# A hybrid decoder block on one core: the recurrence's small transfers move to GpSimd's queue, and SyncE carries loads alone in a fixed order

## The chip, the cores and the metric

The kernel runs on one core of one Trainium2 chip. The metric is the device time of one execution in microseconds. Five instruction streams share the core's SBUF: TensorE (PE; PEld are its weight loads), VectorE (DVE), ScalarE (ACT), GpSimd (POOL) and SyncE (SP). SP and POOL issue DMA transfers here; each engine runs its own stream in order, and an instruction whose input isn't there holds all behind it.

## The reference

One decoder block over 512 tokens of width 2048, in float32. What matters for the change:

```python
mod = c_act @ w_ada[l] + b_ada[l]            # six modulation vectors of 2048
h = rmsnorm(x) * (1 + sc1) + sh1
p = h @ w_in[l]                              # r, k, v of 16 heads, low-rank inputs, 1024 pool columns
y_rwkv = rwkv7_mixer(p[..., :N_RWKV_COLS])   # per head and token: S = S*w + (S a) b^T + v k^T;  y = S r
y_pool = pool_mixer(p[..., N_RWKV_COLS:])    # moving averages over 2, 4, 8, 16 tokens, then a 256x256 matrix
x = x + gt1 * (concat(y_rwkv, y_pool) @ w_out[l])
h = rmsnorm(x) * (1 + sc2) + sh2
x = x + gt2 * conv_ffn(h)                    # gated MLP with a causal convolution of width 3
return rmsnorm(x)
```

## The kernel before, in words

**Stages.** Activations lie transposed: 128 features on the partitions, 512 tokens along the row. Weights arrive as 128x512 float32 blocks (256 KB); `split_weights` (L111) loads one on SP (L113), rounds it to a high part on ACT (L115) and forms the low part on DVE (L117). Each product of two 128x128 by 128x512 blocks is three matmuls (high by high, high by low, low by high). The first stage (to about 160 us) computes half of the modulation, the normed input and the first eight of the 35 column blocks of W_in. The second, the *recurrence* stage, is the one that is changed. After it come the output projection, the MLP and the final norm.

**The recurrence stage** interleaves two things on TensorE. The filler is the rest of the projection: 27 column blocks, each 16 products, so 27 x 48 = 1296 matmuls at L333 (`win_units`), one *unit* each. The other is the recurrence of the 16 heads, taken as 8 pairs of heads, in chunks of 64 tokens. A pair goes through `stage_a` (decay, keys, the scores within a chunk), an inversion of small triangular matrices, `stage_b` (the steps over the 8 chunks) and `post` (group norm, bonus, gate). `recurrence` (L688) writes TensorE's order by hand: it keeps a modelled `clock` in us, each part yields what it takes and how long its results need, and where no part is ready a unit of the projection is put in. `manual_schedule` (L734) binds TensorE to that order. The other engines, SP and POOL among them, are ordered by the scheduler of the language.

**The columns of r, k, v.** `win_pair` (L641) makes the three column blocks of the next pair. `shift` (L234) takes each from PSUM to SBUF (one ACT and one DVE instruction), into a `spill` tile that is stored to DRAM (`sp`, L648); `stage_a` loads it again (L387) into tiles of the rings `ring` (7 buffers) and `v`. The first thing that ACT does with them is a square (L395).

**The small inverses.** The scores of a pair (L448, masked on DVE at L450) contain 64 triangular blocks of 16x16. Eight transfers gather them to DRAM (`dn`, L456), one brings them back with one block per partition (`nl`, L458), DVE inverts all 64 together (28 short instructions at L472 and L474, between L466 and L475), one transfer stores the result (`dx`, L477), and eight scatter it (L479) into `x4w`, a buffer that is zeroed once (L339). ACT copies that to `x4` (L482). All of these transfers are issued by SP. `q.inverted` (L483) is the modelled time at which the inverse is there, 44 us on; `stage_b` waits for it (L525) before its first product with the inverse (L530).

**The second part of the modulation** fills DVE: `ada_rest` (L343) loads 192 blocks of 256 KB (L350) into three `war` buffers and reduces each against a piece of c in `cq` (L348) with one DVE instruction (L351); one is traced at every sixth unit.

**The pooling groups** take their sums over tokens on DVE (`pool_front`, L276) and their matrix on TensorE (`pool_back`, L296); results go to DRAM (`mixd`, L305), as those of the pairs do (L636). `load_mix` (L749) reads them in the next stage.

Of the kernel before, what the change touches and what calls it, by code (L numbers as in the profile page):

```python
# [16 lines left out]
P = 128  # L17
# [11 lines left out]
NB = 10  # L29
NJ = NF // 2  # L30
# [27 lines left out]
def block_kernel(ctx, tc, a, out, stop=None, dbg=None):  # L58
# [52 lines left out]
    def split_weights(src, eng=V):  # L111
        raw = wp.tile([P, WC], F32, tag="wraw", name="wraw", bufs=4)
        nc.sync.dma_start(raw, src)  # L113
        hi = wp.tile([P, WC], F32R, tag="whi", name="whi", bufs=3)
        S.copy(hi, raw)  # L115
        lo = wp.tile([P, WC], F32R, tag="wlo", name="wlo", bufs=3)
        eng.tensor_tensor(lo, raw, hi[:, :].bitcast(F32), op=ALU.subtract)  # L117
        return hi, lo
# [7 lines left out]
    def project(ps, src, acts, start=True, stop=True, engs=(V,)):  # L126

        n = len(acts)
        for k0 in range(0, n, WC // P):
            wh, wl = split_weights(src[:, k0 * P : k0 * P + WC], engs[k0 // 4 % len(engs)])  # L130
# [45 lines left out]
    first = {}  # L176
    p0ctx = ExitStack()
    p0 = p0ctx.enter_context(tc.tile_pool(name="p0", bufs=1))
    if True:
# [28 lines left out]
        for k in range(KT):  # L208
# [14 lines left out]
            for i0 in range(0, 8, WC // P):  # L223
                wh, wl = split_weights(a["win0"][k, :, i0 * P : i0 * P + WC])
                for ii in range(WC // P):
                    sl = slice(ii * P, (ii + 1) * P)
                    mm3(pf[i0 + ii], wh[:, sl], wl[:, sl], *H[k], start=k == 0, stop=k == KT - 1)
        p0ctx.close()
# [4 lines left out]
        if True:  # L233
# [8 lines left out]
            def ring16(name):  # L242
                return ra.tile([P, 16 + T], F32, tag="ring", name=name, bufs=7)
# [3 lines left out]
            S.activation(xwa[0:64, :], xwa[0:64, :], AF.Tanh)  # L247
            xg1 = ra.tile([P, T], F32, tag="xg1", name="xg1")
            shift(pf[1], 25, xg1)
            S.activation(xg1, xg1, AF.Sigmoid)  # L250
            xg2 = ra.tile([P, T], F32, tag="xg2", name="xg2")
            shift(pf[2], 26, xg2)
            S.activation(xg2, xg2, AF.Sigmoid)
# [5 lines left out]
            for i, m in ((3, 0), (4, 8), (5, 16)):  # L259
                t = vtile("v") if i == 5 else ring("rkv")  # L260
# [3 lines left out]
            upad = [ring16("upad") for i in range(2)]  # L264
            for i in range(2):
                V.memset(upad[i][:, 0:16], 0.0)
                S.copy(upad[i][:, 16:], pf[6 + i])
            ps0ctx.close()

    def load_pw(gi):  # L270
        t = ra.tile([P, T], F32, tag="war", name="pw", bufs=3)
# [24 lines left out]
    def pool_back(gi, zs, pw):  # L296
        for d in range(2):
# [6 lines left out]
            if gi:  # L304
                nc.sync.dma_start(mixd[8 + j], mx)  # L305
# [16 lines left out]

    def win_units(fi, ps):

        src = a["win1"][fi - 8, :, :]
# [12 lines left out]
    x4w = ra.tile([P, 8, 2, 64], F32, tag="x4", name="x4w")  # L338
    G.memset(x4w, 0.0)  # L339
    cq = [None]  # L340
    modq = ra.tile([P, 4, 48], F32, tag="modq", name="modq")

    def ada_rest(n0, n1):  # L343
        for n in range(n0, n1):
            kq, j = divmod(n, 48)
            if j == 0:
                cq[0] = ra.tile([P, T], F32, tag="cq", name="cq")
                nc.sync.dma_start(cq[0], cact[0:1, kq * T : (kq + 1) * T].partition_broadcast(P))  # L348
            wa = ra.tile([P, T], F32, tag="war", name="war", bufs=3)
            nc.sync.dma_start(wa, a["ada2"][kq, j, :, :])  # L350
            V.scalar_tensor_tensor(wa, wa, 1.0, cq[0], op0=ALU.mult, op1=ALU.mult,  # L351
                                   accum_out=modq[:, kq, j : j + 1])
# [16 lines left out]
    class Pair:  # L369
        begun = False  # L370

# [9 lines left out]
    def stage_a(p, q):  # L381

        if p:
            rkv = []
            for i in range(3):
                t = vtile("v") if i == 2 else ring("rkv")
                nc.sync.dma_start(t, sp[p, i])  # L387
                rkv.append(t)
        else:
            rkv = rkv0  # L390
        r, k, v = rkv
        lw = ra.tile([P, P], F32, tag="lw", name="lw")
        nc.sync.dma_start(lw, a["lora"][p, :, 0, :])
        sq = ring("sq")
        S.activation(sq, k, AF.Square, scale=col("kk", p))  # L395
        yield 0.0, 4.0
# [10 lines left out]
        S.activation(al, psal, AF.Sigmoid, bias=col("a0", p))  # L407
        tc.keep_in_program_order(S.preload_act_table_set("natural_log_exp_and_others"))
# [3 lines left out]
        mid = ra.tile([P, NL, 1], F32, tag="mid", name="mid", bufs=2)  # L412
# [40 lines left out]
        nl = ra.tile([64, 16, 16], F32, tag="nl", name="nl")  # L453
        dn = tc.dram_tile([64, 16, 16], F32, name=f"dn{p}")
        for b in range(8):
            nc.sync.dma_start(dn[8 * b : 8 * b + 8, :, :].rearrange("s i j -> i s j"),  # L456
                              nt[16 * b : 16 * b + 16, :, 16 * (b % 4) : 16 * (b % 4) + 16])
        nc.sync.dma_start(nl, dn[:, :, :])  # L458
# [5 lines left out]
        V.scalar_tensor_tensor(k2, r, col("rk", p), k2, op0=ALU.mult, op1=ALU.mult)  # L464
        xyl = ra.tile([64, 2, 16, 16], F32, tag="xyl", name="xyl")
        V.tensor_add(xyl[:, 1, :, :], nl, lanei)  # L466
        prod = ra.tile([64, 64], F32, tag="prod", name="prod")
# [9 lines left out]
        nc.sync.dma_start(dx[:, :, :, :], xyl)  # L477
        for b in range(8):
            nc.sync.dma_start(x4w[16 * b : 16 * b + 16, :, :, 16 * (b % 4) : 16 * (b % 4) + 16],  # L479
                              dx[8 * b : 8 * b + 8, :, :, :].rearrange("s w i j -> i s w j"))  # L480
        x4 = q.x4 = ra.tile([P, 8, 2, 64], F32, tag="x4c", name="x4")
        S.copy(x4, x4w)  # L482
        q.inverted = clock[0] + 44.0  # L483
        yield 1.35, 6.0
# [19 lines left out]
    def stage_b(p, q):  # L504
# [20 lines left out]
        yield 1.0, max(2.0, q.inverted - clock[0] - 0.9)  # L525
# [87 lines left out]
    def post(p, q, py, y):  # L613
# [22 lines left out]
        nc.sync.dma_start(mixd[p], rs)  # L636
        yield 1.8, 0.0

    sp, made = {}, {0}
# [43 lines left out]
    clock = [0.0]  # L683
# [4 lines left out]
    def recurrence():  # L688

        units, n, adas = projection(), 0, 0  # L690
# [3 lines left out]
        more = True  # L694
        while True:
# [9 lines left out]
            else:  # L705
                if more:
                    more = next(units, 1) is None
                    if more:
                        clock[0] += 0.23
                        n += 1  # L710
                        if n % 6 == 0:
                            m = min(192, adas + 1)
                            ada_rest(adas, m)
                            adas = m
# [17 lines left out]
        ada_rest(adas, 192)  # L732

    with tc.manual_schedule(engines={mybir.EngineType.PE}):  # L734
# [3 lines left out]
    V.tensor_add(modq[:, 0, :], modq[:, 0, :], modq[:, 1, :])  # L738
    V.tensor_add(modq[:, 2, :], modq[:, 2, :], modq[:, 3, :])
    V.tensor_add(modq[:, 0, :], modq[:, 0, :], modq[:, 2, :])  # L740
    V.tensor_add(mod[:, 32:80], modq[:, 0, :], cols("b_ada", 32, 80))
    V.scalar_tensor_tensor(gsc2, mod[:, 64:80], 1.0, cols("n2", 0, 16), op0=ALU.add, op1=ALU.mult)

# [596 lines left out]
```

## Time and profile before

| | |
|---|---|
| median of 3 runs | 2346.11 us (2345.15 to 2349.61) |
| the profiled execution | 2349.0 us; span from first to last instruction 2347.1 us |
| mean granted TensorE clock | 0.981 |
| busy share of the span | PE 94%, DVE 69%, ACT 43%, POOL 5% |
| recurrence stage, first to last L333 | 163.1 to 761.2 us |
| transfers issued by SP there per pair for the inverses | 8 + 1 + 1 + 8 |

How to read the lines: times are us from the span's start unless they are marked ns. A group line gives line, engine, operation, out<-in, shape and count, then busy us and mean ns of one, then the idle time of the engine before them and what ended it. A wait line gives who waited for whom, us in all, times and the longest. SPq and POOLq are the queues' own instructions. In a stretch, each engine's busy us stand with its count of instructions, then the granted clock, the share of the 16 DMA engines that was busy, and GB/s.

### The profile page before, as it was taken

The numbers are of one execution on the slowest core, as the hardware profiler recorded it, in microseconds if no ns is written. First come the engines' busy times: TensorE is split into PE (matmuls) and PEld (weight loads), VectorE is DVE, ScalarE is ACT, GpSimd is POOL, SyncE is SP. The second block draws the span as 40 slices with busy tenths as digits, with TensorE's granted clock in tenths as the row PEclk, the third lists the DMA queues.
The fourth block names the chain that finished last, engine by engine and source line by source line (L and its number), as shares of the span: only waits on it lengthen the run. The fifth ranks groups of instructions, "written<-read, shape, count | busy, mean of one in ns | idle before, by whom it ended". The sixth has DMA issues, their size and how long they took to land.

```text
span 2347.1 us, 42629 instructions
## 1 busy us (share of the span) xinstructions
PE 2206.0 (94%) x17090; PEld 1958.5 (83%) x17090; DVE 1611.8 (69%) x2543; ACT 1006.5 (43%) x1416; POOL 126.1 (5%) x183
## 2 busy tenths in 40 slices
PE   4778798898899999999999999999999999999997
PEld 3656566666677799999999999999999888888897
DVE  7977786877665366788888877777777645353454
ACT  3243333333333346655555555555555422233353
POOL 0000000000000010111010100000000000110000
PEclk9999899999999999999999999999999999999998
DMA  9966665666533766698888877777776667663464
GB/s 353 339 221 187 210 198 168 202 201 186 151 77 93 251 187 184 204 271 235 250 225 248 234 200 201 199 199 197 200 197 196 221 222 268 226 211 112 124 189 155
DMA packets 200218, 480.77 MB, mean 205 GB/s; under 512 B 46481, under 2 KB 53201, under 8 KB 191825
## 3 DMA queue, kind: packets, MB, share of 16 engines
q1 hardware_dynamic: 180098, 410.91, 53.7%
q0 software_dynamic: 18864, 66.07, 13.7%
q8 instruction: 134, 2.20, 0.4%
q10 hardware_dynamic: 1056, 1.05, 0.1%
q14 instruction: 66, 0.54, 0.1%
HBM read 440.45 MB, written 37.49 MB: 204 GB/s over the span
## 4 chain that ended last, share of the span: by engine, by line
PE 67%; DVE 12%; issue 11%; DMA 8%; ACT 2%; SPq 1%; POOL 0%; DVEq 0%; POOLq 0%; ACTq 0%
PE b L124 18%; PE b L122 18%; PE b L123 18%; PE mm L333 6%; DMA war<-ada 6%; DVE jk L214 3%; DVE war L351 2%; DVE wlo L117 1%; DMA wrow<-wup 1%; PE pa L300 1%; DVE sacc L199 0%; DVE al L151 0%; PE pb L570 0%; ACT ah L150 0%; DMA cq<-cact 0%
## 5 line engine op out<-in xcount | busy, mean ns | idle before, releaser
L124 PE MATMUL b<-t,ulo 128*128 128x256 f32 x1408 | 397.2, 282 | 0.0
L122 PE MATMUL b<-t,uhi 128*128 128x256 f32 x1408 | 396.8, 282 | 0.0
L123 PE MATMUL b<-t,uhi 128*128 128x256 f32 x1408 | 396.7, 282 | 0.0
L115 ACT CAST whi<-wraw 128x512 fp32r<-128x512 f32 x236 | 145.4, 618 | 381.9 <-PE mm L333 222.9
L124 PE MATMUL b<-act,ulo 128*128 128x512 f32 (+1 forms) x880 | 308.0, 350 | 0.0
L123 PE MATMUL b<-act,uhi 128*128 128x512 f32 (+1 forms) x880 | 307.8, 350 | 0.0
L122 PE MATMUL b<-act,uhi 128*128 128x512 f32 (+1 forms) x880 | 307.7, 350 | 0.0
L122 PE MATMUL b<-y,uhi 128*128 128x256 f32 x1056 | 298.1, 282 | 2.1 <-ACT uhi L930 2.1
L124 PE MATMUL b<-y,ulo 128*128 128x256 f32 x1056 | 297.8, 282 | 0.4 <-DVE ulo L932 0.4
L123 PE MATMUL b<-y,uhi 128*128 128x256 f32 x1056 | 297.9, 282 | 0.0
L932 DVE TENSOR_TENSOR ulo<-wd,uhi 128x1024 fp32r<-128x1024 f32 (+1 forms) x120 | 136.2, 1135 | 215.6 <-ACT uhi L930 210.8
L122 PEld LDWEIGHTS b<-t,uhi 128*128 128x128 f32 x1408 | 266.9, 190 | 0.0
L124 PEld LDWEIGHTS b<-t,ulo 128*128 128x128 f32 x1408 | 266.9, 190 | 0.0
L123 PEld LDWEIGHTS b<-t,uhi 128*128 128x128 f32 x1408 | 266.8, 190 | 0.0
L930 ACT CAST uhi<-wquart 128x1024 fp32r<-128x1024 f32 x156 | 163.8, 1050 | 203.8 <-PE b L123 177.5
L930 ACT CAST uhi<-wd 128x1024 fp32r<-128x1024 f32 (+1 forms) x120 | 117.3, 978 | 291.1 <-PE b L123 290.0
L932 DVE TENSOR_TENSOR ulo<-wquart,uhi 128x1024 fp32r<-128x1024 f32 x156 | 190.9, 1224 | 71.9 <-ACT uhi L930 71.9
L117 DVE TENSOR_TENSOR wlo<-wraw,whi 128x512 fp32r<-128x512 f32 x236 | 161.2, 686 | 82.3 <-ACT whi L115 81.5
L930 ACT CAST uhi<-r 128x1024 fp32r<-128x1024 f32 x132 | 138.6, 1050 | 162.8 <-PE b L123 159.2
L932 DVE TENSOR_TENSOR ulo<-r,uhi 128x1024 fp32r<-128x1024 f32 x132 | 161.2, 1222 | 61.8 <-ACT uhi L930 61.7
L122 PEld LDWEIGHTS b<-y,uhi 128*128 128x128 f32 x1056 | 200.2, 190 | 2.5 <-ACT uhi L930 2.5
L124 PEld LDWEIGHTS b<-y,ulo 128*128 128x128 f32 x1056 | 200.1, 190 | 0.6 <-DVE ulo L932 0.6
(302 smaller groups left out, 4455.7 us busy)
## 6 DMA issues: line engine op xcount, KB each, us to landing
wquart<-wup SPq DMA_DIRECT2D x176, 512.0 KB, 4.8
wa<-ada SPq DMA_DIRECT2D x48, 1024.0 KB, 6.9
war<-ada SPq DMA_DIRECT2D x192, 256.0 KB, 3.6
wd<-wdn SPq DMA_DIRECT2D x80, 512.0 KB, 4.0
wraw<-win SPq DMA_DIRECT2D x140, 256.0 KB, 4.2
wraw<-wout SPq DMA_DIRECT2D x96, 256.0 KB, 3.6
wquart<-wup POOLq DMA_DIRECT2D x44, 512.0 KB, 7.3
r<-wup SPq DMA_DIRECT2D x44, 512.0 KB, 4.5
```

The source lines that it names most:

```text
L115: S.copy(hi, raw)
L117: eng.tensor_tensor(lo, raw, hi[:, :].bitcast(F32), op=ALU.subtract)
L122: PE.matmul(ps, wh, xh, start=start, stop=False, skip_group_check=more)
L123: PE.matmul(ps, wh, xl, start=False, stop=False, skip_group_check=more)
L124: return PE.matmul(ps, wl, xh, start=False, stop=stop, skip_group_check=more)
L214: V.scalar_tensor_tensor(jk, wa, 1.0, cb, op0=ALU.mult, op1=ALU.mult, accum_out=mod[:, j : j + 1])
L300: PE.matmul(ps, pw[:, i, d * P : (d + 1) * P], zs[i], start=i == 0, stop=i == 1)
L333: PE.matmul(ps, w[:, sl], x, start=k == 0 and i == 0, stop=k == KT - 1 and i == 2)
L351: V.scalar_tensor_tensor(wa, wa, 1.0, cq[0], op0=ALU.mult, op1=ALU.mult, accum_out=modq[:, kq, j : j + 1])
L930: S.copy(hi[:, 0:n], src)
L932: lo_of[0] = V.tensor_tensor(lo[:, 0:n], src, hi[:, 0:n].bitcast(F32), op=ALU.subtract)
```

## The change

Five things change, all in the recurrence stage or in what leads to it.

1. The transfers of the inverses and the stores of the mix (`dn`, `nl`, `dx`, the scatter, `mixd`) are issued by GpSimd. The yields of `stage_a` are cut anew around them: the gather is traced 2 us after the scores, the way back 5 us after that, and `INV` is 36 us from there. `stage_b` waits until it is set.
2. SP and GpSimd join `manual_schedule`: their order is that in which the program traces them. SP's loads are written ahead by hand: a weight block three blocks ahead (`load_block`), an ada block three ahead (`AHEAD`, four buffers), `lw` in the third column block of its pair. Two ada places are left out after each quarter of 48.
3. r, k, v stay in SBUF: `shift` writes into `rk` (three buffers) or `v` (two), `spill` and `sp` are gone, `ring` has six buffers. The matrices of two pooling groups share `rk`.
4. The scatter writes straight into `x4`, now two buffers that GpSimd zeroes for each pair; the copy at L482 is gone.
5. At the stage's start the first block is split ahead of it, the pooling columns leave PSUM earlier, and the two sigmoids for the gate move into pair 0's `stage_a`.

```diff
+AHEAD = 3
+NQ = 48
+INV = 36.0
-    def split_weights(src, eng=V):
+    def load_weights(src):
         raw = wp.tile([P, WC], F32, tag="wraw", name="wraw", bufs=4)
         nc.sync.dma_start(raw, src)
+        return raw
+
+    def split_weights(raw, eng=V):
...
+    def load_block(i):
+        if i < 27 * 4:
+            blocks.append(load_weights(a["win1"][i // 4, :, i % 4 * WC : (i % 4 + 1) * WC]))
...
     def win_units(fi, ps):
         for k0 in range(0, KT, WC // P):
-            wh, wl = split_weights(src[:, k0 * P : k0 * P + WC])
+            b = blocks.pop(0)
+            wh, wl = b if isinstance(b, tuple) else split_weights(b)
             for kk in range(WC // P):
+                if kk == 1:
+                    load_block((fi - 8) * 4 + k0 // 4 + 3)
...
-            wa = ra.tile([P, T], F32, tag="war", name="war", bufs=3)
-            nc.sync.dma_start(wa, a["ada2"][kq, j, :, :])
-            V.scalar_tensor_tensor(wa, wa, 1.0, cq[0], op0=ALU.mult, op1=ALU.mult,
-                                   accum_out=modq[:, kq, j : j + 1])
+    def load_ada(n):
+        if n < 4 * NQ:
+            t = ra.tile([P, T], F32, tag="war", name="war", bufs=4)
+            nc.sync.dma_start(t, a["ada2"][n // NQ, n % NQ, :, :])
+            was.append(t)
+
+    def ada(n):
+        kq, j = divmod(n, NQ)
+        wa = was.pop(0)
+        V.scalar_tensor_tensor(wa, wa, 1.0, cqs[kq], op0=ALU.mult, op1=ALU.mult, accum_out=modq[:, kq, j : j + 1])
+        load_ada(n + AHEAD)
+        if j == NQ - 1 and kq < 3:
+            load_cq(kq + 1)
...
     def stage_a(p, q):
-            for i in range(3):
-                t = vtile("v") if i == 2 else ring("rkv")
-                nc.sync.dma_start(t, sp[p, i])
-                rkv.append(t)
+        r, k, v = rkvs.pop(p)
+        lw = lws.pop(p)
...
-            nc.sync.dma_start(dn[8 * b : 8 * b + 8, :, :].rearrange("s i j -> i s j"),
-                              nt[16 * b : 16 * b + 16, :, 16 * (b % 4) : 16 * (b % 4) + 16])
-        nc.sync.dma_start(nl, dn[:, :, :])
...
+        yield 1.35, 2.0
+
+        x4 = q.x4 = ra.tile([P, 8, 2, 64], F32, tag="x4", name="x4", bufs=2)
+        G.memset(x4, 0.0)
+        dn = tc.dram_tile([64, 16, 16], F32, name=f"dn{p}")
+        for b in range(8):
+            G.dma_start(dn[8 * b : 8 * b + 8, :, :].rearrange("s i j -> i s j"),
+                        nt[16 * b : 16 * b + 16, :, 16 * (b % 4) : 16 * (b % 4) + 16])
+        yield 0.0, 5.0
+
+        nl = ra.tile([64, 16, 16], F32, tag="nl", name="nl")
+        G.dma_start(nl, dn[:, :, :])
...
-        nc.sync.dma_start(dx[:, :, :, :], xyl)
+        G.dma_start(dx[:, :, :, :], xyl)
         for b in range(8):
-            nc.sync.dma_start(x4w[16 * b : 16 * b + 16, :, :, 16 * (b % 4) : 16 * (b % 4) + 16],
-                              dx[8 * b : 8 * b + 8, :, :, :].rearrange("s w i j -> i s w j"))
-        x4 = q.x4 = ra.tile([P, 8, 2, 64], F32, tag="x4c", name="x4")
-        S.copy(x4, x4w)
-        q.inverted = clock[0] + 44.0
-        yield 1.35, 6.0
+            G.dma_start(x4[16 * b : 16 * b + 16, :, :, 16 * (b % 4) : 16 * (b % 4) + 16],
+                        dx[8 * b : 8 * b + 8, :, :, :].rearrange("s w i j -> i s w j"))
+        q.inverted = clock[0] + INV
+        yield 0.0, 1.0
...
-        yield 1.0, max(2.0, q.inverted - clock[0] - 0.9)
+        yield 1.0, 2.0
+        while q.inverted is None:
+            yield 0.0, 0.5
+        yield 0.0, q.inverted - clock[0]
...
-        nc.sync.dma_start(mixd[p], rs)
+        G.dma_start(mixd[p], rs)
...
     def win_pair(p):
+        rkvs[p] = []
         for i in range(3):
+            if i == 2:
+                load_lw(p)
             ps = mmtile()
             yield from win_units(8 + 3 * (p - 1) + i, ps)
-            t = ra.tile([P, T], F32, tag="spill", name="spill", bufs=2)
+            t = vtile("v") if i == 2 else rktile("rk")
             shift(ps, 8 * i + p, t)
-            d = tc.dram_tile([P, T], F32, name=f"sp{p}_{i}")
-            nc.sync.dma_start(d, t)
-            sp[p, i] = d
+            rkvs[p].append(t)
...
-    with tc.manual_schedule(engines={mybir.EngineType.PE}):
+    with tc.manual_schedule(engines={mybir.EngineType.PE, mybir.EngineType.SP, mybir.EngineType.Pool}):
         recurrence()
```

In the changed kernel's numbering the lines named most are: L333 becomes L355, L351 becomes L377, L426 becomes L449, L450 becomes L473, L466 becomes L497, L530 becomes L562.

More of the change, by code (lines that the diff above doesn't have):

```diff
@@ L227, in block_kernel @@
                     mm3(pf[i0 + ii], wh[:, sl], wl[:, sl], *H[k], start=k == 0, stop=k == KT - 1)
+        for i in range(2):
+            load_block(i)
+        blocks[0] = split_weights(blocks[0])
         p0ctx.close()
@@ L259, in block_kernel @@
             for i, m in ((3, 0), (4, 8), (5, 16)):
-                t = vtile("v") if i == 5 else ring("rkv")
+                t = vtile("v") if i == 5 else rktile("rk")
                 shift(pf[i], m, t)
                 rkv0.append(t)
[L264 to L267, printed above, removed]
             ps0ctx.close()
     def load_pw(gi):
-        t = ra.tile([P, T], F32, tag="war", name="pw", bufs=3)
+        if gi == 3:
+            t = ra.tile([P, T], F32, tag="post", name="pw", bufs=2)
+        else:
+            t = rktile("pw")
         pw = t.rearrange("p (i d) -> p i d", i=2)
@@ L688, in recurrence @@
     def recurrence():
-        units, n, adas = projection(), 0, 0
+        units, n, adas, pause = projection(), 0, 0, 0
         live = dict.fromkeys("dbap")
@@ L694, in recurrence @@
         more = True
+        load_block(2)
+        load_cq(0)
+        for i in range(AHEAD):
+            load_ada(i)
         while True:
```

91 lines of the change are left out of this document (49 added, 42 removed).

## The prediction

> **What bounds the kernel now.** I read the page's slices first, then busy time by stretch, then who waited for whom, then the order of time around single stalls. The stage that the change touches is the one in which L333 runs, 163.1 to 761.2 us.
>
> ```profile
> span 2347.1 us, 42629 instructions
> core 0: us, PE busy (x) PEld busy (x) DVE busy (x) ACT busy (x) POOL busy (x), PEclk, DMA share, GB/s
> 163.10:300.00 136.90, 114.05 (x851) 85.30 (x852) 101.11 (x266) 45.15 (x66) 0.00 (x0) 0.89 0.67 203
> 500.00:645.00 145.00, 130.37 (x1353) 96.49 (x1352) 101.96 (x259) 55.73 (x86) 0.00 (x0) 0.96 0.59 172
> 645.00:761.20 116.20, 115.25 (x1250) 87.99 (x1249) 66.80 (x148) 36.47 (x61) 0.00 (x0) 1.00 0.31 85
> 761.20:2347.10 1585.90, 1565.45 (x11217) 1475.51 (x11215) 1049.90 (x1245) 745.21 (x1011) 123.37 (x172) 0.99 0.70 208
> 163.10:761.20 598.10, 537.29 (x5481) 404.29 (x5482) 424.56 (x1097) 205.52 (x320) 0.00 (x0) 0.95 0.57 168
> ```
>
> TensorE is the bound everywhere; what can be gained is its idle time. After 761.2 it is busy 99% and the change does not touch that part, so I carry it over. In the stage it idles 598.1 - 537.3 = 60.8 us, nearly all before 645. The granted clock of 0.95 costs about 5% of 598, 30 us; part of that falls into idle time, so I count 22. Everything gone would be 60.8 + 22 = 83 us: that is the floor of the time. What stops TensorE:
>
> ```profile
> PE pb L563 <- DVE Tm L560: 15.4, 4, 6.5
> PE pb L601 <- DVE rw L602: 9.6, 10, 1.7
> PE mm L333 <- DVE wlo L117: 8.1, 3, 4.7
> PE pa L426 <- ACT sq L395: 8.0, 1, 8.0
> DVE war L351 <- DMA war<-ada: 73.7, 61, 3.7
> DVE war L351 <- DMA cq<-cact: 6.7, 3, 4.0
> ACT sq L395 <- DMA rkv<-sp: 15.2, 5, 4.4
> ACT x L482 <- DMA x4w<-dx: 8.5, 4, 6.1
> SPq L387 <- DMA sp<-spill: 14.4, 18, 2.0
> ```
>
> (Columns: us in all, times, longest.) TensorE waits mostly for VectorE, and VectorE itself waits 80.4 us for the loads of L350 and L348. Nearly each TensorE stall has such a wait in the 12 us ahead of it (the longest of L563, 6.5 us, has two, together 7.7). So I convert: without the 8.0 us that ScalarE causes, 52.8 us of stalls stand against 80.4 us of VectorE waits, and I price one us of VectorE waiting at 0.6 us of TensorE (52.8/80.4 = 0.66, less what is plain order).
>
> **The change part by part.**
>
> *ScalarE no longer waits for landings.* L482's copy and the reload of r, k, v (L387) go.
>
> ```profile
> 237.06 1.04 ACT L482 COPY x<-x4w 128x1024 f32<-128x1024 f32 x1 [6.12 <-DMA x4w<-dx]
> 240.72 2.07 PE L426 MATMUL pa<-sq,hmat 128*128 128x512 f32 x2 [8.04 <-ACT sq L395]
> sp<-spill SPq DMA_DIRECT2D x21, 256.0 KB, 3.5
> ```
>
> The copy held ScalarE's queue 6.12 us, the square L395 stood behind it, and TensorE stopped 8.04 us. That stall goes whole. The other waits of these two lines, 15.2 + 8.5 - 6.1 = 17.6 us, show in no single stall; a third is taken, 5 us (bounds 0 and 17.6). **Gain 13 us.** The 21 stores and 21 reloads also leave the queue. In their place r, k hold three buffers, v two: a product of the next pair waits for a buffer if stage_a is late. In the built order r of a pair is last read about at the pair's scores, 22 to 101 matmuls of the projection before the next pair's k must have left its PSUM bank; I cost that at nothing. If that cover is gone, the projection stops, us for us.
>
> *The ada loads are paced.* Before, VectorE finished all of L351 early:
>
> ```profile
> core 0: us, DVE busy (x), PEclk, DMA share, GB/s
> 163.10:645.00 481.90, 128.47 (x378) 0.94 0.63 188
> 645.00:761.20 116.20, 0.70 (x2) 1.00 0.31 85
> ```
>
> Now SP has the program's order, two ada loads to one block of W_in, up to unit 1188 of 1296: 0.917 of the stage, or 548 us, in place of 482. So 12% of the ada work and of its waits, 0.12 x (128.5 + 80.4) = 25 us, leave the crowded part for one where VectorE is 57% busy and TensorE loses nothing. At 0.6: **gain 15 us** (bounds 0 and 25).
>
> *Do the ada waits vanish?* A load lands 3.6 us after issue, and issue costs 0.33:
>
> ```profile
> war<-ada SPq DMA_DIRECT2D x192, 256.0 KB, 3.6
> 179.69 0.33 SPq L350 DMA_DIRECT2D war<-ada  x1
> L351 DVE SCALAR_TENSOR_TENSOR war<-war,cq 128x512 f32<-128x512 f32 x184 | 124.3, 686 | 76.0 <-DMA war<-ada 68.7 <-DMA cq<-cact 6.7
> ```
>
> I took VectorE's order in both built programs, priced each instruction by its row, and measured the work between the instruction that frees a load's buffer and its use. The mean is 5.1 us before and 4.95 after. What is missing to 4.0 us sums to 64 before (measured: 73.7) and 100 after. So VectorE still asks for a load about when it lands, four buffers or not, and the waits do not vanish. I leave them as they are, except for the 10 us by which the measured sum exceeds the counted one, which I put down to SP being stuck behind the chain: **gain 6 us**. Bounds: 36 us more waits cost 22; all 80.4 gone give 48.
>
> *The chain moves to GpSimd.* Per pair 18 transfers leave SP, 144 in all, with 14 stores of the mix.
>
> ```profile
> 396.98 3.65 SPq L456 DMA_DIRECT2D dn<-sb  x8
> 402.23 0.45 SPq L458 DMA_DIRECT2D nl<-dn  x1
> 408.16 0.41 DVE L466 TENSOR_TENSOR xyl<-nl,lanei 64x256 f32<-64x256 f32 x1
> 427.16 0.37 DVE L475 COPY xyl<-xyl 64x256 f32<-64x256 f32 x1
> 430.87 4.32 SPq L479 DMA_DIRECT2D x4w<-dx  x8
> 440.59 1.09 PE L530 MATMUL pa<-x,sb 64*64 64x64 f32 x30 [1.57 <-ACT sg L405]
> L847 POOL DMA_DIRECT2D x2d<-x x24 | 13.1, 547 | 786.9 <-DVE x L820 786.1 <-DMA wraw<-wout 0.7
> L1217 POOL DMA_DIRECT2D out<-x x1 | 0.8, 796 | 0.3 <-POOL x L1216 0.3
> L1074 POOL DMA_DIRECT2D wquart<-wup x44 | 37.9, 862 | 620.4 <-DMA wquart<-wup 602.9 <-issue 17.1 <-DMA r<-wup 0.4
> L339 POOL MEMSET x4w<- 128x1024 f32 x1 | 1.0, 955 | 0.0
> nl<-dn SPq DMA_DIRECT2D x8, 64.0 KB, 3.4
> dn<-sb SPq DMA_DIRECT2D x64, 8.0 KB, 1.9
> x2d<-x POOLq DMA_DIRECT2D x16, 128.0 KB, 3.2
> ```
>
> GpSimd has issued no transfer of 64-byte runs, so its price is bounded: 0.55 us (128 rows, L847) below, 0.86 (L1074, accumulating) above; 512 runs cost 0.80 (L1217). I take 0.55 for dn's 128 runs and 0.63 for x4's 256. Landing is bounded by 1.9 and 3.2; I take 2.5. GpSimd is then busy some 158 x 0.6 + 8 x 0.96 = 100 us of 598, no bound. dn and nl take 8 x 0.55 + 2.5 + 0.5 + 3.8 = 11.2 us, where SP had nl landed about 9 to 10 us after its first issue. In the built order VectorE has 10.7, 10.0, 6.2, 5.0, 6.9, 5.7, 5.6 and 7.5 us of work between the masks and the first use of nl; with a fifth of waiting added, the shortfalls to 11.2 sum to about 20 us, where before shows 2.3. At 0.6: **loss 11 us** (bounds 0 and, at 0.86 and 3.9 a landing, 32). The way back, x4's 8 x 0.63 + 2.5 = 7.5 against 4.32 + 2.0, is longer by 1.2 us and saves the copy's 1.04; in the tightest pair shown 440.6 - (430.9 + 4.3 + 2.0) = 3.4 us are free. Cost nothing; if that cover is gone, L562 waits us for us. Behind the waiting nl and dx on GpSimd stand only mix stores, which nobody reads before 761, and the next pair's memset; pair 2's and pair 3's dn stand behind a mix store whose product comes up to 2 matmuls later, some 2 us that the cover takes.
>
> *The clock* follows idle time: 13 + 15 + 6 - 11 = 23 of 60.8 idle go, 38% of 22 is 8, of which I count 6. **Sum: 13 + 15 + 6 - 11 + 6 = 29 us**, 2349.0 to 2320 in the profiled execution, which ran 2.9 us over the median of 2346.1; from that median, **2317 us**.
>
> **The rivals.**
>
> *The loads come early after all* (0.27). If the counting above fails because SP was what delayed them, all 80.4 us go: 48 in place of 6, and the clock gives 12: 13 + 15 + 48 - 11 + 12 = 77 at most, I take 68: **2278**. For it: 14.4 us of SP waiting for its own spills, and dx and nl waits at its head. Against it: the counted 64 already explains most of 73.7.
>
> *A different queue is no different path* (0.10). If what waits are landings and not SP, only ScalarE's 13 us remain, less the 11: 2 us, **2344**, no change. [...]
>
> *GpSimd is late* (0.21, slower). At 0.86 us an issue and 3.9 a landing nl lands 6.9 + 3.9 + 0.9 + 3.9 = 15.6 us after the masks; the shortfalls sum to 54, cost 32; x4 lands some 48 us after them where pair 3 has 440.6 - 397.0 = 43.6, a stop at L562 of about 3 us a pair, 24. Gains of 34 stand against 56: **2368**. It decides from about 0.75 us an issue.
>
> **How the numbers follow.** Forecast 0.42 (2317, own range 2300 to 2335), the others as given. Signs: about 4.7 us (0.2%) is what a measurement here can tell from no change. Faster 0.42 + 0.27 = 0.69, same 0.10, slower 0.21. The range runs from 2268 (some way below 2278, above the floor of 2346 - 83 = 2263) to 2362, short of the worst of the slower case.
>
> **What would show it.** Right: no wait of ScalarE on r, k or x4; no 8 us stall at L449; ada instructions up to the stage's end; war waits of 60 to 90 us still there; VectorE waiting about 2.5 us a pair at L497. Wrong: war waits under 20 us (2278); GpSimd's issues over 0.75 us, or L562 stopping on x4 (2368); a stop of L355 for a buffer of r or k.

## The result, and the profile after

The changed kernel takes **2363.4 us** (median of 4 runs, 2362.5 to 2368.3) against 2347.2 us for the kernel before, run beside it (2345.2 to 2349.6). The ratio is 1.0073, with a 95% interval of 1.0055 to 1.0091: it is slower by 0.7%, some 17 us, where 2317 us and faster was forecast, and it lies just above the range (2362 us). The profiled execution took 2362.6 us, its span 2360.8.

Busy time by stretch, after. The stage now runs from 163.8 to 774.0 us, first to last L355; columns as in the prediction.

```profile
span 2360.8 us, 42543 instructions
163.80:300.00 136.20, 120.01 (x889) 89.50 (x890) 108.68 (x284) 51.22 (x77) 21.81 (x39) 0.95 0.60 177
500.00:658.00 158.00, 131.28 (x1359) 99.03 (x1359) 108.16 (x281) 54.26 (x85) 26.56 (x47) 0.94 0.51 147
658.00:774.00 116.00, 109.98 (x1228) 83.57 (x1227) 72.46 (x176) 32.52 (x55) 14.09 (x25) 1.00 0.43 129
774.00:2360.80 1586.80, 1563.97 (x11216) 1474.13 (x11214) 1049.73 (x1246) 745.75 (x1010) 125.60 (x173) 0.99 0.71 207
163.80:774.00 610.20, 537.58 (x5481) 404.53 (x5482) 424.68 (x1094) 200.82 (x316) 92.47 (x164) 0.96 0.50 145
```

The part behind the stage is the same (1586.8 against 1585.9 us). The stage grew from 598.1 to 610.2 us, 12 us, with TensorE's and VectorE's busy time unchanged (537.6 and 424.7 us), so TensorE idles 610.2 - 537.6 = 72.6 us where it idled 60.8. In the last 116 us it idles 6.0 us where it idled 1. The DMA engines are busy less than before (0.50 of their time against 0.57): over the stage as a whole the loss does not go with busier DMA engines.

What the engines wait for in the stage, after (us in all, times, longest):

```profile
DVE war L377 <- DMA war<-ada: 96.2, 60, 5.4
DVE xyl L497 <- DMA nl<-dn: 18.6, 8, 4.0
...
ACT sq L415 <- DVE rk L250: 26.5, 7, 5.5
...
PE pb L633 <- DVE rw L634: 19.8, 13, 3.5
PE pb L595 <- DVE Tm L592: 12.5, 5, 6.1
...
PE mm L355 <- DVE v L250: 7.9, 1, 7.9
...
PE pa L562 <- DMA x<-dx: 5.0, 2, 2.8
...
SPq L116 <- DVE wlo L123: 297.3, 61, 19.1
```

and SyncE's row for the same load before, where it is L113:

```profile
SPq L113 <- DVE wlo L117: 92.8, 45, 8.4
```

The 8 us stall at L449 is gone, and ScalarE waits for no landing of r or k, and once, 0.5 us, for one of x4. In its place TensorE waits more often for VectorE (38 times and 64.8 us, before 27 times and 46.6), and VectorE waits longer for the ada loads (96.2 us, before 73.7) and for nl (18.6 us). (The 7.9 us of L355 for v end at 163.8 us, where the stage begins; they are no stop inside it and do not count in the 72.6 us or the 64.8.) What has grown most is SyncE's own standing: 297 us at L116, the load of a weight block, until VectorE has read the buffer that the load is to fill, where it was 93 us.

SyncE's issues in order of time, after, shows what that does:

```profile
302.20 1.03 SPq L371 DMA_DIRECT2D war<-ada  x2
308.52 0.33 SPq L116 DMA_DIRECT2D wraw<-win  x1
308.89 1.10 SPq L371 DMA_DIRECT2D war<-ada  x2
319.66 0.33 SPq L116 DMA_DIRECT2D wraw<-win  x1
320.05 0.90 SPq L371 DMA_DIRECT2D war<-ada  x2
```

Block, two ada loads, then nothing for some 5 and 10 us until the next block's buffer is free, and the next two ada loads behind it. I matched each ada load with the end of the instruction that freed its buffer. After, a load is issued 5.2 us later on average (median 4.0); before, 2.0 us (median 0.2). The ada work also ends later: VectorE's last ada instruction starts at 708.7 us, before at 645.2.

```profile
L377 DVE SCALAR_TENSOR_TENSOR war<-war,cq x192: 665/686/694, 158.0 to 708.7; 128x512 f32<-128x512 f32 x192
```

GpSimd's issues and landings, after:

```profile
L510 POOL DMA_DIRECT2D x<-dx x64 | 36.0, 570 | 34.3 <-DMA dx<-xyl 32.4 <-issue 1.9
L489 POOL DMA_DIRECT2D dn<-sb x64 | 33.8, 536 | 163.2 <-DVE sb L473 109.1 <-DVE z L309 53.5 <-DMA mixd<-mxp 0.5
```
```profile
dn<-sb POOLq DMA_DIRECT2D x64, 8.0 KB, 3.8
dx<-xyl POOLq DMA_DIRECT2D x8, 128.0 KB, 4.4
x<-dx POOLq DMA_DIRECT2D x64, 16.0 KB, 4.2
nl<-dn POOLq DMA_DIRECT2D x8, 64.0 KB, 4.1
war<-ada SPq DMA_DIRECT2D x192, 256.0 KB, 4.3
```

An issue costs 0.54 and 0.57 us; a landing of the chain takes 3.8 to 4.4 us, where SyncE's took 1.9 to 3.4. The ada loads land later too, 4.3 against 3.6 us. GpSimd's order of time in pair 1, whose masks were done at 250.5 us:

```profile
246.45 4.51 POOL L510 DMA_DIRECT2D x<-dx  x8 [4.73 <-DMA dx<-xyl]
251.00 0.58 POOL L323 DMA_DIRECT2D mixd<-mxp  x1
252.81 0.56 POOL L323 DMA_DIRECT2D mixd<-mxp  x1 [1.24 <-DMA x<-dx]
253.36 0.97 POOL L486 MEMSET x<- 128x1024 f32 x1
254.26 3.83 POOL L489 DMA_DIRECT2D dn<-sb  x7
```

dn starts 3.8 us late, behind two mix stores, pair 0's x4 and a memset: GpSimd's own fixed order takes part in the delay.

### The profile page after: what moved, and what is told of

Same layout as the page of the kernel before. It is cut to its first block, busy times and chain, and to the rows that moved or that the text cites. A ratio compares the mean times of both kernels' runs of the same rounds, so it can differ in the third digit from the quotient of the medians.

```text
span 2360.8 us, 42543 instructions
## 1 busy us (share of the span) xinstructions
PE 2204.6 (93%) x17090; PEld 1957.3 (83%) x17090; DVE 1612.0 (68%) x2543; ACT 1003.1 (42%) x1410; POOL 220.8 (9%) x348
## 4 chain that ended last, share of the span: by engine, by line
PE 74%; DVE 10%; DMA 9%; issue 2%; ACT 2%; POOL 1%; SPq 1%; DVEq 0%; POOLq 0%; ACTq 0%
PE b L130 20%; PE b L128 20%; PE b L129 20%; PE mm L355 5%; DMA war<-ada 5%; DVE jk L225 2%; DVE war L377 1%; DMA dn<-sb 1%; POOL dn L489 1%; DVE wlo L123 1%; DMA nl<-dn 1%; DMA wrow<-wup 1%; DMA wraw<-win 1%; ACT ah L156 0%; PE pa L318 0%
## 5 line engine op out<-in xcount | busy, mean ns | idle before, releaser
L121 ACT CAST whi<-wraw 128x512 fp32r<-128x512 f32 x236 | 145.2, 618 | 367.8 <-PE mm L355 238.7
L981 ACT CAST uhi<-wquart 128x1024 fp32r<-128x1024 f32 x156 | 163.8, 1050 | 203.6 <-PE b L129 177.3
L377 DVE SCALAR_TENSOR_TENSOR war<-war,cq 128x512 f32<-128x512 f32 x192 | 129.8, 686 | 104.3 <-DMA war<-ada 99.0
```

Of the source, the lines that this page charges most:

```text
L377: V.scalar_tensor_tensor(wa, wa, 1.0, cqs[kq], op0=ALU.mult, op1=ALU.mult, accum_out=modq[:, kq, j : j + 1])
L981: S.copy(hi[:, 0:n], src)
```

## The experiments

**Theory A**: the loss comes from SyncE's fixed order, in which ada loads stand behind a weight block that waits. **Theory B**: it comes from the chain on GpSimd. All ratios are to the kernel before on the same chip, and 0.1% is 2.3 us; an interval is about 0.0015 to either side (0.0018 for the changed kernel), so a difference of two ratios is known to some 5 us.

**SyncE free.** In the changed kernel the list of engines in fixed order loses SyncE.

```diff
-    with tc.manual_schedule(engines={mybir.EngineType.PE, mybir.EngineType.SP, mybir.EngineType.Pool}):
+    with tc.manual_schedule(engines={mybir.EngineType.PE, mybir.EngineType.Pool}):
```

> The changed kernel with SyncE's queue ordered by the scheduler again; TensorE and GpSimd keep their fixed order. Theory A (the loads of ada stand behind a weight-block load that waits at SyncE's head): the mean time from a war buffer's release to its load's issue falls from 5.2 to about 2.0 us as before, VectorE's waits for ada from 95.6 to under 70 us, and the time from 2363 to about 2350. Theory B (GpSimd's chain lands late): nothing of the chain moves, the time stays within 3 us of 2363.

Measured: 2338.8 us, ratio 0.9963 (0.9948 to 0.9978). That is 1.0073 - 0.9963 = 1.1%, **26 us** below the changed kernel, and faster than the kernel before. Ada loads now go out 0.07 us after their buffer's release. VectorE's waits, and SyncE's issues in the same stretch of the span:

```profile
DVE war L377 <- DMA war<-ada: 26.8, 31, 2.4
DVE xyl L497 <- DMA nl<-dn: 17.2, 8, 3.3
```
```profile
302.09 7.69 SPq L371 DMA_DIRECT2D war<-ada  x7
309.91 0.34 SPq L116 DMA_DIRECT2D wraw<-win  x1
311.35 7.84 SPq L371 DMA_DIRECT2D war<-ada  x8
```
```profile
SPq L116 <- DVE wlo L123: 208.4, 83, 11.2
```
```profile
L377 DVE SCALAR_TENSOR_TENSOR war<-war,cq x192: 669/689/699, 158.9 to 481.0; 128x512 f32<-128x512 f32 x192
```

Seven and eight ada loads now go out between two blocks. SyncE still stands 208 us at L116, so the standing by itself is not what costs; what changed is that no ada load waits behind it. The fixed order is most of the loss; the wait for nl has stayed. One edit changes two things here, however: VectorE's order is the scheduler's, and its last ada instruction now starts at 481 us and not at 709. The ada work is no longer spread over the whole stage, and this run cannot tell the late loads from the spreading.

**The chain on GpSimd alone**, in the kernel before: `nc.sync` becomes `G` in the issues of dn, nl, dx and x4w.

> The kernel before with one edit: dn, nl, dx and the eight writes of x4w are issued by GpSimd instead of SyncE. Theory A: SyncE, still ordered freely, loses the waits for dn and dx, so the ada waits stay at or below 74 us; VectorE waits some 18 us for nl instead of 2, and the time is 2347 less up to 6 or plus up to 8. Theory B: the copy of x4w now waits for GpSimd's eight writes, nl comes 4 us later, and the time is 2358 or more.

Measured: 2370.0 us, ratio 1.0098 (1.0084 to 1.0113), 22 us slower, with the ada waits where they were (73.7 us). Theory B holds beside A: the changed kernel suffers from both. VectorE's wait for nl explains only part of these 22 us, since it is 9.0 us in all, before 2.3:

```profile
DVE xyl L466 <- DMA nl<-dn: 9.0, 7, 3.4
```

**Both undone**: SyncE free, the chain and the mix stores on SyncE. What is left of the change is r, k, v in SBUF, the doubled x4, the fourth war buffer, the pauses of ada, loads written ahead of their use, and the new order at the stage's start, which no run tries alone.

```diff
-    with tc.manual_schedule(engines={mybir.EngineType.PE, mybir.EngineType.SP, mybir.EngineType.Pool}):
+    with tc.manual_schedule(engines={mybir.EngineType.PE}):
-            G.dma_start(dn[8 * b : 8 * b + 8, :, :].rearrange("s i j -> i s j"),
+            nc.sync.dma_start(dn[8 * b : 8 * b + 8, :, :].rearrange("s i j -> i s j"),
...
```

> The changed kernel with the chain's transfers and mixd back on SyncE and SyncE ordered by the scheduler: what is left of the change is r, k, v in SBUF, the doubled x4 without a copy, the fourth war buffer and the pace of ada. Theory A: about as without the fixed order alone, 2345 to 2352, nl's waits on VectorE back to some 3 us. Theory B: 8 us or more below the kernel with GpSimd's chain and a free SyncE. If the pace of ada is itself the loss (TensorE idle in the last 116 us of the stage), this stays above 2355.

Measured: **2317.4 us, ratio 0.9872** (0.9857 to 0.9887). It beats both kernels, by 30 us and 46 us. Its stage, and its waits for ada:

```profile
162.70:729.60 566.90, 527.23 (x5481) 399.91 (x5482) 421.30 (x1094) 200.33 (x314) 5.72 (x6) 0.98 0.54 156
```
```profile
DVE war L377 <- DMA war<-ada: 37.5, 36, 4.5
```

TensorE idles 566.9 - 527.2 = 39.7 us. So the way from before to after has three parts, taken in this order: -30 us for all the rest, +21 us (0.9963 - 0.9872) for the chain and the mix stores on GpSimd in a fixed order, +26 us for SyncE's fixed order. They sum to 17 us, the result, as they must; SyncE in a fixed order with the chain still on it was not tried. VectorE's last ada instruction starts at 518 us here.

**Which part of the fixed order?** First, each ada load one step earlier in it (`AHEAD = 4`).

> The changed kernel with AHEAD = 4 instead of 3: with four war buffers each load is placed right behind the ada step that frees its buffer, one ada step (about 2.6 us of the stage) earlier in SyncE's fixed order. Theory A: release to issue falls from 5.2 to about 3 us, the ada waits from 95.6 to 50 to 65 us, the time to about 2352; if instead SyncE now stands at the ada load and the weight blocks come late, TensorE's waits for wlo and whi grow. Theory B: no change, 2360 to 2366.

Measured: ratio 1.0054 (1.004 to 1.0069), 4 us less, which the intervals do not tell from nothing; ada loads still went out 5.1 us after release. A miss: one step does not carry a load past the block it stands behind. Then the blocks later:

```diff
                 if kk == 1:
-                    load_block((fi - 8) * 4 + k0 // 4 + 3)
+                    load_block((fi - 8) * 4 + k0 // 4 + 2)
...
-        load_block(2)
```

> The changed kernel, all three fixed orders kept, but each weight block is loaded two blocks ahead instead of three (the third load at the start is left out), so that its wraw buffer came free one block earlier. Theory A (ada loads stand behind the weight block's wait at SyncE's head): L116's wait for wlo falls from 292 to under 120 us, release to issue of the ada loads from 5.2 to under 2.5 us, and the time to about 2340, as with SyncE free. Rival: the fixed order costs by something else (loads of cq, lw, pw out of place, or the landing that rose to 4.2 us): the time stays above 2355. If two blocks ahead are too few, TensorE and VectorE wait for wraw.

Measured: ratio 1.0061 (1.0045 to 1.0076), and SyncE stands as long as in the changed kernel:

```profile
SPq L116 <- DVE wlo L123: 300.4, 65, 18.5
```

Theory A's expectation failed here. The rows of SyncE's waits name VectorE and not TensorE: a block that is asked for later may only let SyncE run ahead to the next block, where it stands again with ada loads behind it. That reading was put to the test by taking the ada loads out of SyncE's order altogether, with everything else of the change kept:

```diff
             t = ra.tile([P, T], F32, tag="war", name="war", bufs=4)
-            nc.sync.dma_start(t, a["ada2"][n // NQ, n % NQ, :, :])
+            S.dma_start(t, a["ada2"][n // NQ, n % NQ, :, :])
```

> The changed kernel, SyncE, GpSimd and TensorE in their fixed orders, with one edit: the 192 loads of war are issued by ScalarE, whose order the scheduler sets, so that none stands in SyncE's fixed order. Theory A (the fixed order holds the ada loads back; moving the weight block alone did not free them, because SyncE then only runs further ahead to the next block's wait): release to issue falls from 5.2 to under 2 us, the ada waits from 95.6 to under 45 us, the time to 2340 to 2348, some of the gain lost to ScalarE's waits before issues. Rival (the fixed order costs through the weight blocks or VectorE's order, not through ada's place): 2355 or more.

Measured: ratio 0.9981 (0.9973 to 0.999), 22 us below the changed kernel, release to issue 0.8 us.

```profile
DVE war L377 <- DMA war<-ada: 34.7, 39, 2.5
...
ACT whi L121 <- DMA war<-ada: 46.8, 8, 9.7
...
SPq L116 <- DVE wlo L123: 385.2, 89, 19.7
```

SyncE stands at L116 longer than ever, 385 us, and the time is gained all the same. So the place of the ada loads in SyncE's fixed order is some 22 of its 26 us. ScalarE paid with 47 us of waiting at L121 and 57 us in all, which did not undo the gain. The last ada instruction starts at 627 us, again earlier than in the changed kernel, so how much of the 22 us is late loads and how much is ada work spread to 709 us stays open.

**Which part of the chain?** From the version with both undone, the first half on GpSimd again, or the second:

```diff
-            nc.sync.dma_start(dn[8 * b : 8 * b + 8, :, :].rearrange("s i j -> i s j"),
+            G.dma_start(dn[8 * b : 8 * b + 8, :, :].rearrange("s i j -> i s j"),
...
-        nc.sync.dma_start(nl, dn[:, :, :])
+        G.dma_start(nl, dn[:, :, :])
```

> The version with SyncE free and the chain on SyncE (2317), with the first half of the chain, dn and nl, back on GpSimd; dx, x4 and mixd stay on SyncE. If GpSimd's 21 us come from VectorE standing at nl (17 us of waits against 3, at 0.6 of TensorE about 10, and more of the clock), most of it comes back here: 2330 to 2338, xyl waits about 17 us. If they come from x4's way back, this stays within 5 us of 2317.

Measured: ratio 0.9967 (0.9954 to 0.9979), 0.95% above the version with both undone, 22 us: as much as the whole chain. VectorE's wait:

```profile
DVE xyl L497 <- DMA nl<-dn: 23.0, 8, 6.0
```

> The version with SyncE free and dn and nl on SyncE, with only dx, x4 and mixd on GpSimd. x4's way back had room to spare, so the slower landing should cost nothing, and SyncE loses its wait for dx: ada loads issue within 0.5 us of release, 0.984 to 0.988 of before. If x4's way back does cost, 0.990 or more, with waits at L562.

Measured: dx, x4 and mixd alone on GpSimd give 0.9923 (0.991 to 0.9935), 12 us above the same version, and TensorE stops for x4:

```profile
PE pa L562 <- DMA x<-dx: 4.1, 3, 2.0
```

Each half costs something alone, and the two together no more than the first. The way back is not free, then; behind a late nl its lateness adds nothing. From dx's issue to the last landing of x4 it takes 11.4 us on average here and 9.2 with both undone. But the waits at L562 grow only from 1.1 to 4.1 us; where the other 9 of the 12 us come from is not shown.

**Is it GpSimd, or any other queue?** dn and nl issued by ScalarE (`S.dma_start`), whose place in order the scheduler sets.

> The version with SyncE free and the chain on SyncE (0.987 of before), with dn and nl issued by ScalarE. GpSimd there cost 22 us (0.997 of before). If that was GpSimd's slower landing (dn 3.8 us against 1.9 from SyncE), ScalarE's transfers land as SyncE's do, VectorE's waits at xyl stay under 8 us, and only ScalarE's issues and its wait for dn cost: 0.987 to 0.992. If any queue but SyncE's costs it (the scheduler no longer knows when nl lands), the xyl waits are near 20 us again and the ratio near 0.996.

Measured: 0.9946 (0.9933 to 0.996), 17 us above. This does not decide cleanly, since ScalarE stood for 73 us itself until dn had landed (37.4 at L121 and 21.0 at L249 the most of it), but the landings speak. The same 64 transfers of dn, issued by SyncE (both undone), by ScalarE and by GpSimd (first half on GpSimd, whose own order is fixed there):

```profile
dn<-sb SPq DMA_DIRECT2D x64, 8.0 KB, 1.6
```
```profile
dn<-sb ACTq DMA_DIRECT2D x64, 8.0 KB, 2.7
```
```profile
dn<-sb POOLq DMA_DIRECT2D x64, 8.0 KB, 2.9
```

By these medians ScalarE's landing is nearly as late as GpSimd's; the last section takes them apart. In these runs the issuer moved the median landing of dn by 1.1 us (ScalarE) and 1.3 us (GpSimd) against SyncE's 1.6, and the versions took 0.7% and 0.95% longer.

**What does a microsecond of VectorE cost at nl?** In the version with both undone, the addition that makes xyl is done six times instead of once.

```diff
-        V.tensor_add(xyl[:, 1, :, :], nl, lanei)
+        for _ in range(6):
+            V.tensor_add(xyl[:, 1, :, :], nl, lanei)
```

> The same version with the addition that makes xyl done six times instead of once: 5 x 0.412 us of VectorE more ahead of each pair's inverse, 16.5 us in the eight, about what VectorE waits there more for GpSimd's nl; the values are the same. By the prediction's price, 0.6 us of TensorE for one of VectorE, it is 10 us slower (0.992); if a microsecond of VectorE in this place costs the stage one or more (GpSimd's dn and nl cost 22 us for 20 of waiting), 17 to 22 us (0.995 to 0.997).

Measured: 0.9948 (0.9934 to 0.9962).

```profile
L498 DVE TENSOR_TENSOR xyl<-nl,lanei x48: 406/411/419, 213.8 to 659.2; 64x256 f32<-64x256 f32 x48
```

40 additions of 0.411 us, 16.4 us of VectorE, cost 0.0076 of 2347 us, 18 us (14 us against the same version with `AHEAD = 4`, below): **about 1 us each, not 0.6**; with the intervals some 0.8 to 1.4 by the first comparison and 0.6 to 1.15 by the second. For the ada waits the price between SyncE free and fixed is far lower: 96.2 - 26.8 = 69 us more of waiting cost 26 us, 0.37 each. It is no constant of these waits, though: below, ada as before in the version with both undone brings 15 us more of them and costs 17 us.

Later in program order did not take the wait away:

```diff
-        yield 0.0, 5.0
+        yield 0.0, 9.0
```

> SyncE free, chain on GpSimd, and the step that takes nl is put 9 instead of 5 clock units after dn, x4's due time moving with it. If GpSimd's 21 us come from VectorE standing at xyl for nl (17.2 us, 0.6 us of TensorE each), those waits go and the time falls from 2339 to about 2329. If they come from the length of the chain up to x4, it rises by some 4 us for each of the 8 pairs that has no slack, 2339 to 2350, with new waits at L562.

Measured, against SyncE free: 0.9984 (0.9972 to 0.9997), 5 us slower, xyl waits still 17.0 us. A miss: VectorE's order is the scheduler's and took the addition no later relative to nl. It says nothing on the price.

**Where the 30 us come from.** x4 written directly, in the kernel before; then r, k, v in SBUF there; then both:

```diff
-        x4 = q.x4 = ra.tile([P, 8, 2, 64], F32, tag="x4c", name="x4")
-        S.copy(x4, x4w)
+        x4 = q.x4 = ra.tile([P, 8, 2, 64], F32, tag="x4", name="x4", bufs=2)
+        G.memset(x4, 0.0)
```

> The kernel before with x4 in two zeroed buffers, written by the eight transfers directly; ScalarE's copy is gone, nothing else is changed. The prediction's term: the 8.0 us stall at L449 and some 5 us of ScalarE's other waits go, about 2334. Rival: the stall moves to the next thing that pair waits for, 2344 or more.

```diff
-                t = vtile("v") if i == 2 else ring("rkv")
-                nc.sync.dma_start(t, sp[p, i])
...
-            t = ra.tile([P, T], F32, tag="spill", name="spill", bufs=2)
+            t = vtile("v") if i == 2 else rktile("rk")
```

> The kernel before with r, k and v kept in three rk and two v buffers (ring of six instead of seven), their way through DRAM gone; nothing else is changed. The prediction gave this edit nothing by itself. If the transfers of r, k, v were what held SyncE and VectorE (SyncE stood 20 us for spill, ada loads behind), the ada waits fall from 73.7 to under 55 us and the time to 2335 or less; if a projection now stands for an rk buffer, L333 waits and the time rises above 2350.

> The kernel before with two edits together: x4 written directly into two zeroed buffers and r, k, v kept in SBUF. Alone they gave 0.9985 and 0.9996. If ScalarE's waits for landings are one cost that needs both (a copy of x4w and the first square of k stand in the same queue), together they give the predicted 13 us, 0.9945; if they add up, 0.998.

Measured: 0.9985 (0.9973 to 0.9996), 0.9996 (0.9985 to 1.0007) and together 0.9982 (0.9969 to 0.9995), 4 us in all. With x4 direct alone the stall is still there, at the same matmul, and 6.5 us long where it was 8.0; what stood behind the copy in ScalarE's order, the exponential at L414, now waits for VectorE, and the square, which TensorE waits for, comes next:

```profile
PE pa L424 <- ACT sq L393: 6.5, 1, 6.5
```
```profile
236.40 0.64 ACT L414 ACTIVATE ep<-cs 128x520 f32<-128x520 f32 x1 [5.37 <-DVE cs L412]
237.21 0.72 ACT L393 ACTIVATE sq<-rkv,vec 128x512 f32<-128x512 f32 x1 [0.17 <-DMA rkv<-sp]
```

With both edits the stall is gone from the trace, and the gain is 4 us all the same.

The other parts, ada as before in the version with both undone (three buffers, loads at their use, no pauses), the fourth buffer alone in the kernel before, and weight blocks loaded at their use:

```diff
-AHEAD = 3
+AHEAD = 0
...
-            t = ra.tile([P, T], F32, tag="war", name="war", bufs=4)
+            t = ra.tile([P, T], F32, tag="war", name="war", bufs=3)
...
+        load_ada(n)
         wa = was.pop(0)
```

> The version with SyncE free and the chain on SyncE (2317), with ada as in the kernel before: three war buffers, each load written just ahead of its use, no pauses. If the 30 us that this version gains on the kernel before come from ada (the fourth buffer, the loads written three steps ahead, the pauses), the ada waits return from 37.5 to about 74 us and the time to 2338 to 2345. If they come from the rest (x4 direct, r, k, v, weight blocks written ahead), it stays below 2325.

Measured: 0.9944 (0.993 to 0.9958), so ada's new form is worth 0.0072, 17 us; its waits return to 52.6 us, from 37.5.

```diff
-            wa = ra.tile([P, T], F32, tag="war", name="war", bufs=3)
+            wa = ra.tile([P, T], F32, tag="war", name="war", bufs=4)
```

> The kernel before with a fourth war buffer (mid in one buffer and prod in 56 columns pay for it); loads are still written just ahead of their use. If the fourth buffer by itself is what frees VectorE, the ada waits fall from 73.7 to about 40 us and the time from 2347 to about 2330; if the place at which the load is written decides, nothing moves by more than 3 us.

Measured: 0.9971 (0.9961 to 0.998), 7 us; ada waits 49.2 us.

```diff
-                if kk == 1:
-                    load_block((fi - 8) * 4 + k0 // 4 + 3)
...
+            i = (fi - 8) * 4 + k0 // 4
+            if i > 1:
+                load_block(i)
             b = blocks.pop(0)
```

> The version with SyncE free and the chain on SyncE (0.987 and, with AHEAD = 4, 0.989 of before) with each weight block's load written at its use again, as before the change. If writing the blocks three ahead is the part of the gain that ada (17 us), x4 and r, k, v (4 us) leave open, the time rises by some 8 us to 0.991; if the scheduler moves the loads forward anyway, nothing changes: 0.986 to 0.990.

Measured: 0.9909 (0.9895 to 0.9924), 9 us above the version with both undone; 5 us above the same with `AHEAD = 4`:

> The version with SyncE free and the chain on SyncE (0.987 of before) with AHEAD = 4. With SyncE free the loads already go out 1.1 us after their buffer's release, so writing them one step earlier should change little: 0.985 to 0.988, ada waits 30 to 38 us.

Measured: 0.9887 (0.9873 to 0.99), no gain over `AHEAD = 3`. So 17 us from ada, 5 to 9 from writing the blocks ahead, and 4 from x4 and r, k, v make up the 30 within their intervals, which leaves room for a few us of the untried start of the stage.

## Why the prediction was wrong, step by step

- **"Do the ada waits vanish?", gain 6 us: this step failed.** It held that SyncE is freed when the chain leaves it, and put SyncE's new fixed order at nothing. SyncE was not freed: its order put the ada loads behind L116's wait, and they went out 5.2 us after their buffers came free, before 2.0. Taking the fixed order away brings 26 us, and taking only the ada loads out of it 22. SyncE's 93 us at the load of a weight block stood in the profile before, and the prediction does not use them.
- *The count under that step* gave 100 us of waits after, and the profile has 96.2: that is luck. It took a load to go out when its buffer comes free. By that rule the trace after has 8.8 us of VectorE's work on average between a buffer's release and its use, not 4.95, and what is missing to 4.0 us sums to 12 us, not 100 (before: 5.7 us and 57, near the 5.1 and 64 that were counted). Only with a buffer freed three uses earlier, where the kernel has four, does it come near: 6.3 us and 85. The waits come from the late issue. The bound of 22 us for 36 us more of waits was near the truth for the same reason, by chance.
- **"The chain moves to GpSimd", loss 11 us: direction right, size wrong.** The shortfall at nl was put at some 20 us and measured 18.6; issues were put at 0.55 and 0.63 us and measured 0.54 and 0.57. Landing was put at 2.5, bounded by 3.2, and measured 3.8 to 4.2. But the loss was 21 us. One part is the price: at about 1 us each and not 0.6, the 17.2 - 3.1 = 14 us more of waiting for nl make up some 14 us. The rest is not settled; with the chain alone on GpSimd, 7 us more of waiting for nl went with 22 us.
- *x4's way back at nothing* was wrong alone: with the mix stores it costs 12 us, and only beside a late nl does it add nothing. It was put 1.2 us longer, without dx's own landing, which rose from 3.2 to 4.4 us. From dx's issue to the last landing of x4 it takes 12.9 us on average, before 9.2: more than the 3.4 us that were free.
- **"ScalarE no longer waits for landings", 13 us:** seen in the profile, the stall at L449 is gone, but worth 4 us. To book the whole stall was the error: what stood behind the copy waits for the next thing. r, k, v buffers at nothing was right (0.9996 alone).
- **"The ada loads are paced", 15 us:** the pace came, to 709 us, about as forecast; the gain is not seen. The versions that are faster end their ada work sooner: at 481 us with SyncE free, 518 with both undone, 627 with ada on ScalarE, and ada's new form, worth 17 us there, ends at 518 us where the old one ends at 578. That is no gain of pace. "TensorE loses nothing" was wrong: with ada in its last 116 us TensorE idles 6.0 us in place of 1, and 2.1 with SyncE free.
- **The clock**, 6 us: it did not follow idle time from before to after. TensorE idles 12 us more, the clock is 0.96 where it was 0.95, and the busy time is the same. In the version with 39.7 us idle it is 0.98, and the busy time 10 us less.
- The rival **GpSimd is late** gave 2368 us, near the result. Its landing of 3.9 us came true, its issues above 0.75 us did not, and the fixed order's 26 us were in no case of mine, so its number is near by chance. **The loads come early** had the effect right (waits fall to 26.8 us with SyncE free) and the wrong sign for this change, which takes freedom from SyncE. **A different queue is no different path** fails by the runs that move one queue's work: they differ by 12 to 26 us.
- That the version with both undone takes 2317 us, the number forecast, is chance: its terms are others.

What stays open: how the fixed order's 26 us divide between late loads and ada work spread over the stage, what the chain costs beyond the wait for nl, and the part that GpSimd's own fixed order and the pauses of ada have in their terms.

## What to carry to other kernels

Before writing a fixed order for a queue, list what each waiting transfer holds up behind it: a load that must wait for a buffer should not stand ahead of loads whose buffers are free, and here leaving that queue to the scheduler was worth 26 us. Price a microsecond of waiting by the place it stands in, not by a mean over all stalls. A count that meets the measured sum is not yet the cause: look in the trace whether its premise, here that a load goes out when its buffer comes free, holds.

## What the runs showed of the hardware

The time from issue to landing of the same strided 8 KB transfer depended on who issued it, and mostly while the ada loads ran. Medians of the transfers of dn, split at the last issue of an ada load, in the three versions with SyncE's order free that are compared above:

| issuer | while ada loads ran | after the last one |
|---|---|---|
| SyncE | 1.7 us | 1.5 us |
| ScalarE | 3.2 us | 1.7 us |
| GpSimd | 4.2 us | 2.0 us |

The DMA engines were busy 0.67 of the time in the first part and 0.28 in the second (GpSimd's version). In the changed kernel the ada loads run to 704 us, all 64 transfers of dn fall among them, and the median is 3.8. Why SyncE's own transfers land only 0.2 us later while the ada loads ran, where ScalarE's land 1.5 and GpSimd's 2.2 us later, is not shown.

After the last ada load GpSimd's median landing is 0.5 us behind SyncE's, and ScalarE's 0.2. While the loads ran the distances were 2.5 and 1.5 us.
